# The delta rule's values turned on VectorE and through DRAM, and the diagonal blocks' substitution cut into steps

## The chip, the cores and the metric

One core of a Trainium2 chip runs the whole program. The metric is the device time of one execution in microseconds (us); the kernel before takes 2083.51 us (median of three runs, 2082.48 to 2084.71).

## The reference

One encoder layer on 256 tokens of width 2048, all in f32: a mixer, a cross-attention into 256 memory tokens and a squared-ReLU MLP, each behind an RMSNorm. The mixer has two branches, retention (8 heads) and a gated delta rule (16 heads of 128 keys and 128 values), whose gated outputs are added and projected. The part that the change touches is the delta rule, evaluated in chunks of 64 tokens:

```
gqkv = silu(causal_conv(gqkv, conv_w));  gq, gk, gv = split(gqkv)
gq, gk = l2_normalize(gq) * GDN_DK**-0.5, l2_normalize(gk)
m = where(strict, (k*beta) @ k.T * decay, 0)          # per head and chunk, 64 x 64
t = triangular_solve(eye + m, eye)                    # unit lower triangular
u = t @ (v * beta);  w = t @ (k * beta * exp(cum_g))
v_new = u - w @ state;  o = (q * exp(g)) @ state + (q @ k.T * decay) @ v_new
state = state * exp(g_last) + (k * exp(g_last - g)).T @ v_new
```

## The kernel before

The weights are streamed. `fetch` takes 1 MB of a weight matrix into one of three `raw` buffers by a DMA on SP's queue (L98), and then, for each half of it, ScalarE writes a rounded copy `whi` (L108) and VectorE the remainder `wlo` (L111). Three buffers of each take halves in turn. TensorE multiplies from those: `blocks` (two blocks of 128 output features by all 256 tokens, two matmuls for each block and 128 inputs, L193 and L194) and `chunk` (128 tokens by 512 features, three matmuls, L151 to L153). A fetch of `blocks` feeds 16 pairs of L193 and L194. After each half `blocks` and `chunk` call `step()`, which runs the first generator in the list `steps` up to its next `yield`; `finish_steps()` runs all to their ends. The order in which each engine takes its instructions is set when the program is built, by a planner that goes by priorities and by times of its own; weights' DMAs, roundings and remainders have the highest priority there.

The mixer runs four groups (`j` = 0 to 3; four delta-rule heads and two retention heads each), in a loop at the end of the mixer: `gdn_stream(j)`, `gdn_blocks`, for `j` over 0 `gate_delta_rule(j - 1)`, then `retention(j)` and `gate_retention(j)`. The delta rule's core `gdn_core(j)` is a generator whose steps run inside `gate_retention(j)`, for group 0 inside `gdn_stream(1)`.

`gdn_stream` works on two pairs of heads. For each pair `blocks` runs over the columns of q, k and v; each result goes through `conv_silu` (a scaled copy on ScalarE, L566, three multiply-adds on VectorE, L569, SiLU on ScalarE, L571). The values `vt` come out with features on partitions and tokens along the row. q and k go through Gram matmuls (L614 to L618), from which `alt` is made (L638, L641), and small copies on ScalarE spread its blocks over `cmp_l`, `pair32` and `pair64` (L646 to L653). For each head TensorE turns `vt` by two transposes into PSUM (L657), and ScalarE evacuates them, scaled by the key's norm `nk`, into `r4`, tokens on partitions (L660).

`gdn_blocks` inverts the 32x32 diagonal blocks of all four heads at once: `cmp_l` goes through DRAM into `lw` (L667, L670), VectorE substitutes 31 columns, two instructions each (L678, L680), on 32 partitions, and the result `tw` goes through DRAM into `ct` (L682, L688), is turned by VectorE's 32x32 transposes into `cu` (L690) and copied into `t64`, `u64` and `u128`. It is called once, and its instructions stand together behind `gdn_stream` in the program. `gdn_core` combines the blocks (L709 and on) and multiplies by `r4` (L742 and on).

Of the kernel before, what the change touches and what calls it, by code (L numbers as in the profile page):

```python
# [17 lines left out]
P = 128  # L18
D = 2048
S = 256  # L20
# [31 lines left out]
def trunk(ctx: ExitStack, tc: tile.TileContext, x, mem, positions, norm_mix_g, w_in, conv_w, gdn_a_log, gdn_dt_bias,  # L52
# [508 lines left out]
    t64, u64, u128 = sparse("t64", 64), sparse("u64", 64), sparse("u128", NT, P)  # L561


    def conv_silu(blk, ps, dst):
        acc = mx.tile([P, S], F32, name="acc", tag="acc", bufs=2)
        act.activation(acc, ps, AF.Copy, scale=cw[:, 3, blk:blk + 1])  # L566
        for j in range(2, -1, -1):
            d = 3 - j
            vec.scalar_tensor_tensor(acc[:, d:], ps[:, :S - d], cw[:, j, blk:blk + 1], acc[:, d:],  # L569
                                     op0=ALU.mult, op1=ALU.add)  # L570
        act.activation(dst, acc, AF.Silu)  # L571

    def diag(alt):
        return alt.rearrange("p a n -> p (a n)")[:, 0:512].rearrange("p (t n) -> p t n", t=NT)[:, :, 0:P]
# [1 line left out]
    def gdn_stream(grp):  # L576

        heads = []
        qe4 = mx.tile([P, 4, NT], F32, name="qe4", tag="qe4", bufs=2)
        for pr in range(2):  # L580
            h0 = grp * 4 + pr * 2
            dec = mx.tile([P, 2, 384], F32, name="dec", tag="dec", bufs=1)
            nc.sync.dma_start(dec, dec_d[h0:h0 + 2].rearrange("h p n -> p h n"))
            kq = mx.tile([P, 2, 2, S], F32, name="kq", tag="kq", bufs=1)
            vts = []
            for part, c0, bofs in ((1, C_GQ, 0), (0, C_GK, 16), (2, C_GV, 32)):
                def evac(b, ps, part=part, bofs=bofs):
                    if part < 2:
                        conv_silu(bofs + h0 + b, ps, kq[:, b, part, :])
                    else:  # L590
                        vt = mx.tile([P, S], F32, name="vt", tag="vt", bufs=2)
                        conv_silu(bofs + h0 + b, ps, vt)
                        vts.append(vt)
                blocks(h1, w_in[0], c0 + h0 * GD, 2, evac)
            if pr == 0:
                finish_steps()
                cmp_l = mx.tile([P, 8, 32], F32, name="cmp_l", tag="cmp", bufs=1)
                r4 = mx.tile([P, 4, NT, GD], F32, name="r4", tag="r4", bufs=1)
            grams = []
            ssk = mx.tile([P, 2, NT], F32, name="ssk", tag="ssk", bufs=2)  # L600
            for b in range(2):
                kh = mx.tile([P, 2, S], F32R, name="kh", tag="kh", bufs=2)
                kl = mx.tile([P, 2, S], F32R, name="kl", tag="kl", bufs=2)
                sq = mx.tile([P, S], F32, name="sq", tag="acc", bufs=2)
                act.activation(kh, kq[:, b], AF.Copy)
                vec.tensor_sub(kl, kq[:, b], kh.bitcast(F32))
                act.activation(sq, kq[:, b, 1], AF.Square)
                g0, g1 = bank(), bank()
                g0v = g0.rearrange("p (a n) -> p a n", a=2)
                g1v = g1[:, 0:256].rearrange("p (a n) -> p a n", a=2)  # L610
                if b == 0:
                    ssq = g1[:, 256:260].rearrange("p (b i) -> p b i", b=2)
                for t in range(NT):
                    pe.matmul(ssq[:, b, t:t + 1], sq[:, t * P:(t + 1) * P], ones[:, :1], start=True, stop=True)  # L614
                for n, (l, r) in enumerate(((kh, kh), (kh, kl), (kl, kh))):
                    pe.matmul(g0v, l[:, 0, 0:P], r, start=n == 0, stop=n == 2)  # L616
                for n, (l, r) in enumerate(((kh, kh), (kh, kl), (kl, kh))):
                    pe.matmul(g1v, l[:, 0, P:S], r[:, :, P:S], start=n == 0, stop=n == 2)  # L618
                grams.append((g0v, g1v))
                for t, src in enumerate((g0v[:, 0, 0:P], g1v[:, 0, :])):  # L620
                    dj = sm.tile([P, S], F32, name="dj", tag="bo", bufs=2)[:, :P]
                    vec.scalar_tensor_tensor(dj, src, 1.0, ident, op0=ALU.mult, op1=ALU.mult,
                                             accum_out=ssk[:, b, t:t + 1])
            ske = mx.tile([P, 2, NT], F32, name="ske", tag="ske", bufs=2)
            vec.tensor_scalar(ske, ssk, EPS, None, op0=ALU.add)
            vec.tensor_scalar(qe4[:, 2 * pr:2 * pr + 2, :], ssq, EPS * GD, EPS * EPS * GD,
                              op0=ALU.mult, op1=ALU.add)
            sc = mx.tile([P, 2, NT], F32, name="sc", tag="sc", bufs=2)
            vec.reciprocal(sc, ske)
            vec.tensor_mul(sc, sc, beta[:, :, h0:h0 + 2].rearrange("p t h -> p h t"))  # L630
            nk = mx.tile([P, 2, NT], F32, name="nk", tag="nk", bufs=2)
            pool.tensor_tensor(nk.rearrange("p b t -> p (b t)"), ske.rearrange("p b t -> p (b t)"), half_pow[:, :4], op=ALU.pow)
            for b in range(2):
                h, slot = h0 + b, pr * 2 + b
                g0v, g1v = grams[b]

                alt = mx.tile([P, 2, 384], F32, name="alt", tag="alt", bufs=4)
                vec.scalar_tensor_tensor(alt[:, :, 0:S], g0v, sc[:, b, 0:1],  # L638
                                         dec[:, b, 0:256].unsqueeze(1).to_broadcast([P, 2, 256]),
                                         op0=ALU.mult, op1=ALU.mult)  # L640
                vec.scalar_tensor_tensor(alt[:, :, S:384], g1v, sc[:, b, 1:2],  # L641
                                         dec[:, b, 256:384].unsqueeze(1).to_broadcast([P, 2, P]),
                                         op0=ALU.mult, op1=ALU.mult)
                for q in range(4):
                    ps_ = slice(32 * q, 32 * q + 32)
                    act.activation(cmp_l[ps_, 2 * slot:2 * slot + 2, :], diag(alt)[ps_, :, 32 * q:32 * q + 32], AF.Copy)  # L646

                for t in range(NT):
                    for a in range(2):
                        to, at = 64 * t + 32 * a, 64 * a  # L650
                        act.activation(pair32[to:to + 32, slot, to:to + 32],
                                       diag(alt)[at:at + 32, t, at + 32:at + 64], AF.Copy)
                    act.activation(pair64[64 * t:64 * t + 64, slot, 64 * t:64 * t + 64], diag(alt)[0:64, t, 64:P], AF.Copy)  # L653

                vps = bank()
                for t in range(NT):
                    pe.transpose(vps[:, t * P:(t + 1) * P], vts[b][:, t * P:(t + 1) * P], ident)  # L657
                r = r4[:, slot, :, :]
                for t in range(NT):
                    act.activation(r[:, t, :], vps[:, t * P:(t + 1) * P], AF.Copy, scale=nk[:, b, t:t + 1])  # L660
                heads.append(alt)
        return heads, cmp_l, r4, qe4

    def gdn_blocks(heads, cmp_l):

        scr_l = dram.tile([P, 256], F32, name="scr_l", tag="scr_l", bufs=2)
        nc.sync.dma_start(scr_l, cmp_l.rearrange("p g n -> p (g n)"))  # L667
# [3 lines left out]
        tw = mx.tile([32, 32, 32], F32, name="tw", tag="tw", bufs=1)  # L671
        vec.memset(tw, 0.0)
        vec.memset(tw.rearrange("p i c -> p (i c)")[:, ::33], 1.0)
        for j in range(31):
            n = 31 - j
            pr = mx.tile([32, 272], F32, name="pr", tag="pr", bufs=2)
            pv = pr[:, :n * (j + 1)].rearrange("p (i c) -> p i c", i=n)
# [7 lines left out]
        for t in range(NT):  # L685
            for a in range(2):
                at = 64 * t + 32 * a
                nc.sync.dma_start(ct[at:at + 32], scr_t[16 * a + t:16 * a + 16:2, :].rearrange("g (i c) -> i g c", i=32))  # L688
        cu = mx.tile([P, 8, 32], F32, name="cu", tag="cu", bufs=1)
        vec.transpose(cu.rearrange("p g c -> p (g c)"), ct.rearrange("p g c -> p (g c)"))  # L690
        for t in range(NT):
            for w in range(2):
# [3 lines left out]
                for a in range(2):  # L696
                    at, to = 64 * t + 32 * a, 64 * a + 32 * w
                    act.activation(u128[to:to + 32, :, t, to:to + 32], cu[at:at + 32, 4 * w:4 * w + 4, :], AF.Copy)
        return ct, cu

    def gdn_core(ct, cu, heads, r4, qe4, yg):

        def couple(lhs, rhs, n):
# [3 lines left out]
                pe.matmul(pv[:, i, :], lhs[:, i, :], rhs[:, i, :], start=True, stop=True)  # L709
            return ps, pv  # L710

        ps, pv = couple(pair32, ct[:, 0:4], 32)
        for at in range(0, P, 32):
            (act.copy if at < 64 else vec.tensor_copy)(pair32[at:at + 32, :, at:at + 32], pv[at:at + 32])
        yield
        ps, pv = couple(pair32, cu[:, 4:8], 32)
        nu = mx.tile([P, 2, P], F32, name="nu", tag="g_w", bufs=1)
        vec.tensor_scalar(nu[:, 0], ps, -1.0, None, op0=ALU.mult)
# [161 lines left out]
    gate_retention, gate_delta_rule = gates()  # L880
    for j in range(5):
        if j < 4:
            heads, cmp_l, r4, qe4 = gdn_stream(j)
            solved = gdn_blocks(heads, cmp_l)
        if j:
            if j < 4:
                quad = mx.tile([P, 4, S], F32, name="mg", tag="mg", bufs=3)
# [5 lines left out]
        if j < 4:  # L893
            yr = mx.tile([P, NT, 512], F32, name="yr", tag="yr", bufs=1)
            yg = mx.tile([P, NT, 512], F32, name="yg", tag="yg", bufs=1)
            retention(j, yr)
            core = gdn_core(*solved, heads, r4, qe4, yg)
            if j:
                steps.append(core)
            gate_retention(j, yr)  # L900
# [216 lines left out]
```

## Time and profile before

| | us |
|---|---|
| median of three runs (range) | 2083.51 (2082.48 to 2084.71) |
| the profiled execution, its own time | 2083.63 |
| its span, first to last instruction | 2081.9 |
| TensorE busy in the span | 2064.7 |
| VectorE busy | 1400.9 |
| ScalarE busy | 1119.2 |

The profile is one execution recorded by the hardware profiler. Matmuls are pipelined: the record of one is longer than the distance to the next one's start, so what a matmul costs is read from the distance between starts, and the busy time of a group counts overlapped time in full. A wait is time in which an engine was idle before an instruction, put down to the work that released it. Idle time of an engine off the path costs nothing. Stages: memory tokens and set-up up to about 190 us, the mixer's four groups up to about 1060, output projection and cross-attention up to 1350, the MLP behind it.

### The profile page before, as it was taken

How to read it: one execution, taken by the hardware profiler on the slowest of the kernel's cores; microseconds unless marked ns; L12 is line 12 of the kernel's file. 1: busy time of each engine (PE TensorE's matmuls, PEld its weight loads, DVE VectorE, ACT ScalarE, POOL GpSimd, SP SyncE). 2: the span in 40 equal slices, each digit the busy share in tenths (PEclk: the TensorE clock that was granted, in tenths of full speed). 3: DMA queues.
4: the chain of work that ended last, by engine and by line, in shares of the span. 5: the costliest groups of instructions: out<-in, count | busy, mean ns of one | idle time of the engine just before them, and what ended most of it. 6: DMA issues, size and time to landing. Idle time of an engine off the chain costs nothing.

```text
span 2081.9 us, 28577 instructions
## 1 busy us (share of the span) xinstructions
PE 2064.7 (99%) x11028; PEld 1780.3 (86%) x11028; DVE 1400.9 (67%) x2226; ACT 1119.2 (54%) x1843; POOL 30.7 (1%) x37
## 2 busy tenths in 40 slices
PE   8999999999999999999999999999999999999998
PEld 6888888888888888888888899888888888888887
DVE  5766879778757885778557665766556546645655
ACT  7684664675547555655446564654444434434444
POOL 0000000000000000000000000000000000000000
PEclk9999999999999999999999999999999999999999
DMA  8787655556555655555467654666566556656653
GB/s 297 236 273 251 196 190 195 168 177 196 185 163 189 195 177 166 186 187 190 155 213 238 193 190 144 187 198 195 190 195 189 194 190 192 192 196 188 193 192 142
DMA packets 314168, 405.11 MB, mean 195 GB/s; under 512 B 18336, under 2 KB 222128, under 8 KB 313904
## 3 DMA queue, kind: packets, MB, share of 16 engines
q1 hardware_dynamic: 313744, 402.77, 60.1%
q8 instruction: 86, 1.41, 0.3%
q10 hardware_dynamic: 288, 0.52, 0.1%
q14 instruction: 50, 0.41, 0.1%
HBM read 389.61 MB, written 13.65 MB: 194 GB/s over the span
## 4 chain that ended last, share of the span: by engine, by line
PE 97%; DMA 1%; ACT 1%; SPq 1%; DVE 0%; issue 0%; POOLq 0%; POOL 0%; ACTq 0%; DVEq 0%
PE s L193 33%; PE s L194 17%; PE s L152 14%; PE s L153 14%; PE s L151 14%; PE b L709 1%; PE b L616 1%; DMA xc<-x 1%; PE b L742 1%; PE b L122 0%; PE b L121 0%; PE b L123 0%; SPq L312 0%; ACT dec_w L521 0%; PE b L618 0%
## 5 line engine op out<-in xcount | busy, mean ns | idle before, releaser
L111 DVE TENSOR_TENSOR wlo<-raw,whi 128x1024 fp32r<-128x1024 f32 x700 | 855.4, 1223 | 515.4 <-ACT whi L108 508.9
L108 ACT ACTIVATE whi<-raw 128x1024 fp32r<-128x1024 f32 x700 | 740.7, 1059 | 689.1 <-PE s L153 342.8
L193 PE MATMUL s<-q,whi 128*128 128x512 f32 x3072 | 1056.8, 390 | 0.3 <-DVE q L1006 0.3
L194 PE MATMUL s<-q,wlo 128*128 128x256 f32 x3072 | 840.6, 281 | 0.8 <-DVE wlo L111 0.8
L193 PEld LDWEIGHTS s<-q,whi 128*128 128x128 f32 x3072 | 567.7, 188 | 109.9 <-DVE q L1006 0.5
L194 PEld LDWEIGHTS s<-q,wlo 128*128 128x128 f32 x3072 | 576.2, 188 | 14.2 <-DVE wlo L111 2.6
L152 PE MATMUL s<-wlo,q 128*128 128x512 f32 x1264 | 495.8, 392 | 0.7 <-DVE wlo L111 0.7
L153 PE MATMUL s<-whi,q 128*128 128x512 f32 x1264 | 492.1, 390 | 0.0
L151 PE MATMUL s<-whi,q 128*128 128x512 f32 x1264 | 451.5, 390 | 2.8 <-ACT q L275 2.8
L151 PEld LDWEIGHTS s<-whi,q 128*128 128x128 f32 x1264 | 237.3, 188 | 52.1 <-ACT q L275 3.2
L152 PEld LDWEIGHTS s<-wlo,q 128*128 128x128 f32 x1264 | 237.7, 188 | 49.5 <-DVE wlo L111 2.2
L153 PEld LDWEIGHTS s<-whi,q 128*128 128x128 f32 x1264 | 237.7, 188 | 47.5
L200 ACT ACTIVATE bo<-s 128x256 f32<-128x256 f32 x192 | 72.8, 379 | 119.4 <-PE s L194 106.2
L201 DVE TENSOR_TENSOR bo<-bo,s 128x256 f32<-128x256 f32 x192 | 80.0, 417 | 44.8 <-ACT bo L200 44.4
L569 DVE SCALAR_TENSOR_TENSOR acc<-bo,cw,acc 128x255 f32<-128x255 f32 (+1 forms) x144 | 66.8, 480 | 3.1 <-ACT acc L566 1.2
L678 DVE TENSOR_TENSOR pr<-lw,tw 32x31 f32<-32x31 f32 (+15 forms) x124 | 40.5, 326 | 10.4 <-DMA lw<-scr_l 8.3
L680 DVE TENSOR_TENSOR tw<-tw,pr 32x31 f32<-32x31 f32 (+15 forms) x124 | 40.6, 327 | 2.0
L1045 DVE SCALAR_TENSOR_TENSOR res<-s,rstd3q,res 128x512 f32<-128x512 f32 (+1 forms) x32 | 22.3, 736 | 11.9 <-PE s L153 11.9
L843 ACT ACTIVATE gth<-s 128x512 f32<-128x512 f32 x32 | 19.0, 592 | 20.3 <-PE s L153 15.1
L1034 DVE SCALAR_TENSOR_TENSOR hs<-bo 128x256 f32<-128x256 f32 x64 | 27.1, 423 | 1.1
L1037 DVE TENSOR_TENSOR q<-hs,q 128x256 fp32r<-128x256 f32 x64 | 26.8, 418 | 0.8 <-ACT q L1036 0.8
L1036 ACT ACTIVATE q<-hs 128x256 fp32r<-128x256 f32 x64 | 26.2, 410 | 0.0
(306 smaller groups left out, 1083.6 us busy)
## 6 DMA issues: line engine op xcount, KB each, us to landing
raw<-w_in SPq DMA_DIRECT2D x143, 1024.0 KB
raw<-w_ff SPq DMA_DIRECT2D x128, 1024.0 KB
raw<-w_xkv SPq DMA_DIRECT2D x31, 1024.0 KB
raw<-w_out SPq DMA_DIRECT2D x16, 1024.0 KB
raw<-w_xq SPq DMA_DIRECT2D x16, 1024.0 KB
raw<-w_xo SPq DMA_DIRECT2D x16, 1024.0 KB
dec_d<-dec_w SPq DMA_DIRECT2D x8, 384.0 KB
dec<-dec_d SPq DMA_DIRECT2D x8, 384.0 KB
```

The source lines that it names most:

```text
L108: rounding = act.activation(hi, src, AF.Copy)
L111: vec.tensor_sub(lo, src, hi.bitcast(F32))
L151: pe.matmul(o, xh, wh, start=first, stop=False)
L152: pe.matmul(o, xh, wl, start=False, stop=False)
L153: pe.matmul(o, xl, wh, start=False, stop=last)
L193: pe.matmul(ps[b], lh, xhl, start=kk == 0, stop=False)
L194: pe.matmul(ps[b][:, :S], ll, xh, start=False, stop=kk == KT - 1)
L200: act.activation(o, ps[b][:, S:], AF.Copy)
L201: vec.tensor_add(o, o, ps[b][:, :S])
L569: vec.scalar_tensor_tensor(acc[:, d:], ps[:, :S - d], cw[:, j, blk:blk + 1], acc[:, d:], op0=ALU.mult, op1=ALU.add)
L678: vec.tensor_mul(pv, lw[:, j, j + 1:32].unsqueeze(2).to_broadcast([32, n, j + 1]), tw[:, j, 0:j + 1].unsqueeze(1).to_broadcast([32, n, j + ...
L680: vec.tensor_sub(tw[:, j + 1:32, 0:j + 1], tw[:, j + 1:32, 0:j + 1], pv)
```

## The change

`conv_silu` gets a flag for the values: SiLU is written back into `acc`, and VectorE's 32x32 transposes (`vec.transpose`, 128x256) put each 32x32 block, turned in itself, into `vt`. Four DMAs for a pair of heads write `vt` into a DRAM tile `v_d` with the blocks in their places, and one DMA reads it back into `r4` with tokens on partitions. TensorE's transposes (L657), their PSUM bank and ScalarE's evacuations (L660) go. The scaling by `nk` is done later, by eight ScalarE instructions on `r4` in the second step of `gdn_core`; `nk` of both pairs is kept in `nk4`. `gdn_blocks` becomes a generator that is put into `steps`; it yields twice ahead of the first column, before every third column and twice after the DMAs into `ct`, and hands its results to `gdn_core` through the list `solved`.

```diff
-    def conv_silu(blk, ps, dst):
+    def conv_silu(blk, ps, dst, blocks_of=False):
...
-        act.activation(dst, acc, AF.Silu)
+        act.activation(acc if blocks_of else dst, acc, AF.Silu)
+        if blocks_of:
+            vec.transpose(dst, acc)
...
+        nk4 = mx.tile([P, 4, NT], F32, name="nk4", tag="nk4", bufs=2)
...
-            vts = []
+            vt = mx.tile([P, 2, S], F32, name="vt", tag="vt", bufs=1)
...
-                        vt = mx.tile([P, S], F32, name="vt", tag="vt", bufs=2)
-                        conv_silu(bofs + h0 + b, ps, vt)
-                        vts.append(vt)
+                        conv_silu(bofs + h0 + b, ps, vt[:, b], blocks_of=True)
...
+            v_d = dram.tile([2, S, GD], F32, name="v_d", tag="v_d", bufs=2)
+            for a in range(4):
+                nc.sync.dma_start(v_d[:, :, 32 * a:32 * a + 32].rearrange("h (b i) f -> i (h b) f", i=32),
+                                  vt[32 * a:32 * a + 32].rearrange("i h (b f) -> i (h b) f", f=32))
+            nc.sync.dma_start(r4[:, 2 * pr:2 * pr + 2], v_d.rearrange("h (t p) f -> p h t f", p=P))
...
-                vps = bank()
-                for t in range(NT):
-                    pe.transpose(vps[:, t * P:(t + 1) * P], vts[b][:, t * P:(t + 1) * P], ident)
-                r = r4[:, slot, :, :]
-                for t in range(NT):
-                    act.activation(r[:, t, :], vps[:, t * P:(t + 1) * P], AF.Copy, scale=nk[:, b, t:t + 1])
...
-    def gdn_blocks(heads, cmp_l):
+    def gdn_blocks(cmp_l, solved):
...
+        yield
+        yield
         for j in range(31):
+            if j % 3 == 2:
+                yield
...
                 nc.sync.dma_start(ct[at:at + 32], scr_t[16 * a + t:16 * a + 16:2, :].rearrange("g (i c) -> i g c", i=32))
+        yield
+        yield
...
-        return ct, cu
+        solved.extend((ct, cu))
+        yield
...
+        ct, cu = solved
         ps, pv = couple(pair32, ct[:, 0:4], 32)
...
         yield
+
+        for i in range(4):
+            for t in range(NT):
+                act.activation(r4[:, i, t, :], r4[:, i, t, :], AF.Copy, scale=nk4[:, i, t:t + 1])
...
-            solved = gdn_blocks(heads, cmp_l)
+            solved = []
+            steps.append(gdn_blocks(cmp_l, solved))
...
-            core = gdn_core(*solved, heads, r4, qe4, yg)
+            core = gdn_core(solved, heads, r4, nk4, qe4, yg)
```

## Rows read from the trace of the kernel before

**Rows 1.** Windows by stage: stretch, length, busy us of engines, granted clock, DMA share, GB/s.
```profile
0.00:190.00 190.00, 181.08 (x913) 150.11 (x914) 124.16 (x204) 129.27 (x263) 2.67 (x9) 1.00 0.82 268
190.00:1060.00 870.00, 870.00 (x4624) 749.52 (x4623) 654.29 (x1210) 496.61 (x898) 25.55 (x24) 1.00 0.56 183
```

**Rows 2.** Waits of TensorE, whole span: who waited for whom, us in total, times, longest.
```profile
PE s L194 <- DVE wlo L111: 0.8, 2, 0.4
```

**Rows 3.** Timeline of TensorE at one head pair's transposes: start, us, line, tiles, count.
```profile
255.74 0.39 PE L193 MATMUL s<-q,whi 128*128 128x512 f32 x1
...
256.08 0.39 PE L193 MATMUL s<-q,whi 128*128 128x512 f32 x1
256.31 0.38 PE L657 MATMUL b<-ident,vt 128*128 128x128 f32 x2
...
256.99 0.38 PE L657 MATMUL b<-ident,vt 128*128 128x128 f32 x2
257.13 0.48 PE L193 MATMUL s<-q,whi 128*128 128x512 f32 x1
...
257.56 0.39 PE L193 MATMUL s<-q,whi 128*128 128x512 f32 x1
```

**Rows 4.** Groups by line: count, busy us, mean ns of one, idle before and its releaser.
```profile
L657 PE MATMUL b<-ident,vt 128*128 128x128 f32 x32 | 6.1, 271 | 0.0
...
L660 ACT ACTIVATE r<-b,nk 128x128 f32<-128x128 f32 x32 | 9.6, 366 | 0.1
...
L690 DVE STREAM_TRANSPOSE cu<-ct 128x256 f32<-128x256 f32 x4 | 1.8, 445 | 0.1
```

**Rows 5.** Timeline of ScalarE behind the Gram matmuls, group 0's first pair.
```profile
254.42 1.06 ACT L108 ACTIVATE whi<-raw 128x1024 fp32r<-128x1024 f32 x1
...
257.72 0.62 ACT L660 ACTIVATE r<-b,nk 128x128 f32<-128x128 f32 x2
...
260.55 1.06 ACT L108 ACTIVATE whi<-raw 128x1024 fp32r<-128x1024 f32 x1
```

**Rows 6.** Timeline of VectorE, at the values' convolution and behind Rows 5.
```profile
246.97 1.22 DVE L111 TENSOR_TENSOR wlo<-raw,whi 128x1024 fp32r<-128x1024 f32 x1 [1.15 <-ACT whi L108]
249.56 0.29 DVE L622 SCALAR_TENSOR_TENSOR dj<-b,ident 128x128 f32<-128x128 f32 x1 [1.37 <-PE b L616]
...
261.64 1.22 DVE L111 TENSOR_TENSOR wlo<-raw,whi 128x1024 fp32r<-128x1024 f32 x1 [2.17 <-ACT whi L108]
```

**Rows 7.** Timeline of TensorE: the first matmuls that read that remainder.
```profile
263.56 0.40 PE L194 MATMUL s<-q,wlo 128*128 128x256 f32 x2
```

**Rows 8.** Waits of SP's DMA queue, mixer (190 to 1060 us).
```profile
SPq L98 <- DVE wlo L111: 303.5, 60, 9.5
...
SPq L688 <- DMA scr_t<-tw: 11.6, 4, 4.0
...
SPq L670 <- DMA scr_l<-cmp_l: 6.2, 4, 3.4
```

**Rows 9.** Timeline of SP: transfers issued around the end of a substitution, and one fetch.
```profile
313.57 0.39 SPq L98 DMA_DIRECT2D raw<-w_in  x1
...
363.27 0.83 SPq L688 DMA_DIRECT2D ct<-scr_t  x2
...
530.29 0.34 SPq L682 DMA_DIRECT2D scr_t<-tw  x1
534.73 1.79 SPq L688 DMA_DIRECT2D ct<-scr_t  x4
```

**Rows 10.** Windows of one us: DMA share and GB/s at the ends of two transfers.
```profile
317.00:318.00 1.00, 1.00 (x7) 0.88 (x6) 0.90 (x4) 0.55 (x1) 0.00 (x0) 1.00 1.03 384
318.00:319.00 1.00, 1.00 (x6) 0.83 (x5) 1.00 (x2) 0.51 (x1) 0.00 (x0) 1.00 0.12 40
...
537.00:538.00 1.00, 1.00 0.54 80
```

**Rows 11.** Timeline of TensorE: the core of group 0 begins.
```profile
371.42 0.97 PE L709 MATMUL b<-ct,pair 128*128 128x32 f32 x8
```

More of the change, by code (lines that the diff above doesn't have):

```diff
@@ L630, in gdn_stream @@
             vec.tensor_mul(sc, sc, beta[:, :, h0:h0 + 2].rearrange("p t h -> p h t"))
-            nk = mx.tile([P, 2, NT], F32, name="nk", tag="nk", bufs=2)
+            nk = nk4[:, 2 * pr:2 * pr + 2, :]
             pool.tensor_tensor(nk.rearrange("p b t -> p (b t)"), ske.rearrange("p b t -> p (b t)"), half_pow[:, :4], op=ALU.pow)
@@ L653, in gdn_stream @@
                     act.activation(pair64[64 * t:64 * t + 64, slot, 64 * t:64 * t + 64], diag(alt)[0:64, t, 64:P], AF.Copy)
-                vps = bank()
-                for t in range(NT):
-                    pe.transpose(vps[:, t * P:(t + 1) * P], vts[b][:, t * P:(t + 1) * P], ident)
-                r = r4[:, slot, :, :]
-                for t in range(NT):
-                    act.activation(r[:, t, :], vps[:, t * P:(t + 1) * P], AF.Copy, scale=nk[:, b, t:t + 1])
                 heads.append(alt)
-        return heads, cmp_l, r4, qe4
-    def gdn_blocks(heads, cmp_l):
+        return heads, cmp_l, r4, nk4, qe4
+    def gdn_blocks(cmp_l, solved):
         scr_l = dram.tile([P, 256], F32, name="scr_l", tag="scr_l", bufs=2)
@@ L698, in gdn_blocks, with gdn_core @@
                     act.activation(u128[to:to + 32, :, t, to:to + 32], cu[at:at + 32, 4 * w:4 * w + 4, :], AF.Copy)
-        return ct, cu
-    def gdn_core(ct, cu, heads, r4, qe4, yg):
+        solved.extend((ct, cu))
+        yield
+    def gdn_core(solved, heads, r4, nk4, qe4, yg):
         def couple(lhs, rhs, n):
@@ L882, in trunk @@
         if j < 4:
-            heads, cmp_l, r4, qe4 = gdn_stream(j)
-            solved = gdn_blocks(heads, cmp_l)
+            heads, cmp_l, r4, nk4, qe4 = gdn_stream(j)
+            solved = []
+            steps.append(gdn_blocks(cmp_l, solved))
         if j:
```

## Prediction

> **What bounds the kernel now.** I read the windows by stage first. In the mixer (190 to 1060 us), the only stage that the change touches, TensorE is busy 870.00 of 870.00 us at a granted clock of 1.00, while VectorE has 654.29, ScalarE 496.61 and the DMA engines a share of 0.56 [rows 1]. Overlapping records can hide small holes, so the list of TensorE's waits comes next: over the whole span its waits on VectorE's remainders come to 0.8 us in two waits [rows 2], and the same list cut to the mixer is empty. So in this stage the end is set by the sum of TensorE's own instructions, and nothing that VectorE, ScalarE or the DMAs give up shortens it. Two things count: how many us of TensorE's row the change takes away, and whether anything that it adds makes a weight half come late. The third reading is therefore TensorE's timeline where the removed transposes stand [rows 3], and the last ones are the places where a half is nearly late [rows 5 to 7] and SP's waits, behind which the weights are fetched [rows 8, 9].
>
> **What is removed from TensorE.** 32 transposes (4 groups, 2 pairs, 2 heads, 2 token halves). Their cost is read as distances between starts. Without anything in between, a pair of L193 and L194 takes from 255.74 to 256.08, 0.34 us. From 256.08 to 257.56 there are three pairs and four transposes in 1.48 us [rows 3]. Three pairs alone take 1.02, so four transposes with both returns to the weights' stream cost 0.46, or 0.115 each. The start at 257.13 shows that part of it is the return: that matmul's record is 0.48 long beside 0.39 for the others. The other heads stand in the stream in the same way. 32 x 0.115 = **3.7 us** less. The upper end is the group's busy time, 6.1 us [rows 4], which counts overlap with the neighbours in full; the lower end is 0, if something else comes late. I take the distances, since they are what TensorE's row is made of.
>
> The record of one transpose is 271 ns [rows 4]. The Trainium skill (TensorE: Matmul & The Clock Gate, Part 4: PE-mode transpose) gives some 275 ns for one in a kernel's context, and the trace agrees as a duration; by that price the estimate would be 32 x 0.275 = 8.8 us, and by the distances of rows 3 it is 3.7.
>
> **ScalarE.** 32 evacuations of 366 ns go (9.6 us busy [rows 4]), 32 scalings of the same 128x128 shape come, read from SBUF. No row shows this form from SBUF; its ends are the rounding's pace, 1.06 us for 1024 columns [rows 5], so 0.13 for 128, and the evacuation's own 366 ns, and I take the latter, so nothing is won or lost in sum. Their place is better than before: between two roundings at 254.42 and 260.55 [rows 5] ScalarE does only small copies for 5 us, among them four of the removed evacuations in two rows of 0.62. The remainder behind it starts at 261.64 and ends at 262.86, and TensorE wants it at 263.56 [rows 6, 7]: 0.7 us to spare, among the tightest places of the mixer. The change takes 1.2 us out of that burst. The eight scalings land in the core's second step, 8 x 0.366 = 2.9 us; if they stood in one piece ahead of a rounding with 0.7 us to spare they would cost 2.2 us once, in group 0, whose core runs among convolutions. Roundings have the higher priority, so I take 0, and 2.2 for the range.
>
> **VectorE.** 16 transposes of 128x256 at 445 ns (the same form as L690 [rows 4]) add 7.1 us to 654. They fall at the values' convolution, where VectorE stands idle for 1.15 and 1.37 us in front of two instructions [rows 6]; that is the cover for two times 0.445. A transpose now waits for the SiLU on ScalarE, and behind it on VectorE's queue are remainders: without the cover a pair would lose 0.9 us less the slack, up to 0.2 us for each of 8 pairs, 1.6 in all. I take 0.
>
> **SP and the DMAs.** For each pair five transfers come into SP's queue behind the values, 40 in all: four of 64 KB in runs of 128 bytes (512 runs each), and the load of `r4`, which waits for all four. While it waits, the fetches behind it in SP's queue wait too, and so, later, roundings and TensorE. How long: the four `ct` loads, 4 x 256 runs of 128 bytes, start at 534.73 [rows 9] and their traffic ends within the window that ends at 538 [rows 10], 3.3 us. Twice as many runs take between 3.3 us (if latency is most of it) and 6.6. The room: a fetch issued at 313.57 [rows 9] has its bytes in by about 318.2, where a share of 0.12 is left [rows 10], so 4.6 us; two other buffers hold 2 x 16 x 0.34 = 11 us of work, so SP can be late by about 6.4. The kernel before has such blocks already, on `scr_t` up to 4.0 us and on `scr_l` up to 3.4 [rows 8], and TensorE waits for none of them; SP mostly waits for buffers to come free, up to 9.5 us at a time. Cost 0; at the upper end 8 x 0.2 = 1.6 us. The traffic itself, 8 times at most 6.6 us and 256 KB of reading, meets a DMA share of 0.56.
>
> **The substitution in parts.** The same 62 VectorE instructions a group, spread by hand over the 16 steps of `retention(0)` or `gate_delta_rule`, where the planner now spreads them. Nothing is removed from TensorE; price 0. Who waits is the core: group 0's `ct` loads are issued at 363.27 and its first matmul starts at 371.42 [rows 9, 11], 8 us later. The two empty steps at each end shift this by at most 4 steps of 8 pairs, 4 x 8 x 0.34 = 11 us, 3 beyond the slack, if the columns in between run no earlier; they are placed earlier than that (the 16 steps end with `retention(0)`, a `gate_retention` before the core), so 0, and 3 for the range. In groups 1 to 3 a whole `retention` lies in between. The steps' yields cost no engine time.
>
> **Sum.** 2083.63 us of the profiled execution less 3.7 = **2079.9**; this execution lies 0.1 above the median. That is 0.17% below, just under the 0.2% (4.2 us) that a measurement of this kernel can tell from no change.
>
> **Rivals.**
> 1. *The gain is eaten by small waits.* VectorE's 1.6, ScalarE's 2.2 and a part of SP's 1.6 come true instead of 0: 2079.9 + 3.1 to 5.4, about 2083.5. For it: spare times of 0.7 us; against it: an empty list of waits today although ScalarE's burst was longer.
> 2. *Weights come late behind the new load on SP.* Place: the fetch behind `r4`'s load, 8 times. Rows show runs of 128 bytes only into SBUF; written to DRAM they may be dearer. At one and a half times the 6.6 us the block is 9.9, 3.5 beyond the room, 8 x 3.5 = 28 us: 2108. It decides from (4.2 + 3.7) / 8 = 1.0 us beyond the room, a block of 7.4 us. Against it: fetches have the higher priority when the planner orders SP's queue, and the blocks of today, up to 4.0 us [rows 8], cost nothing. The Trainium skill (DMA: Bandwidth & Descriptors, Specifications) has a rule for this side: below 512 bytes a transfer is read, modified and written. No run here shows a write of that size yet.
> 3. *Removing a transpose gives more than its distance.* By the busy time of 6.1 us the time is 2077.5; by the full records, 32 x 0.271 = 8.7 us, it is 2074.9. Against it: the neighbours run under those records. The skill's duration named above would give the same as the records.
> 4. *The change does not do what it says*: the steps alter nothing, since the planner had spread the columns already. That is in the forecast.
>
> **How the numbers follow.** Forecast 0.67, of which 0.20 falls on the far side of 4.2 us, as the price of a transpose need only be 0.131 instead of 0.115, or the runs differ by half a us (the three runs span 2.2 us); rival 1 0.12; rival 2 0.10; rival 3 0.11. Faster by over 0.2%: 0.20 + 0.11 = 0.31; within: 0.47 + 0.12 = 0.59; slower: 0.10. The range takes in the busy time of 6.1 less half a us for the runs' spread below (2077.0) and rival 1 above (2084.0); it leaves out rival 2 and the far part of rival 3.
>
> **What would show it.** In the profile after: TensorE's busy time and matmul count down by some 6 us overlapped and 32; the distances around the convolutions back at 0.34; TensorE's list of waits in the mixer still empty (a row for L194 or L152 on `wlo` is rival 1, one with roundings waiting for a `raw` DMA is rival 2); SP's waits gaining a row of eight waits on `v_d`, each under 6.4 us; transposes of 0.445 us on VectorE. The prediction is wrong if TensorE's instructions in the mixer get shorter by other than 3 to 4.5 us, or if it waits there for over 1 us.

## The result and the profile after

| | us |
|---|---|
| before, median of six runs | 2083.52 |
| changed, median of six runs (range) | 2094.31 (2091.77 to 2096.13) |
| ratio | 1.005, 95% interval 1.004 to 1.006 |
| changed, the profiled execution | 2091.77, span 2090.0 |

The change makes the kernel 10.8 us slower; the forecast was 3.6 us faster. The profiled execution is the fastest of the six, 8.1 us of span above that of before.

Windows by stage (columns as in rows 1) show where it lies:

```profile
0.00:190.00 190.00, 181.31 (x919) 150.31 (x920) 124.44 (x204) 129.25 (x264) 2.74 (x9) 1.00 0.83 270
190.00:1070.00 880.00, 871.25 (x4594) 746.27 (x4593) 660.64 (x1226) 496.97 (x899) 24.59 (x24) 1.00 0.58 186
```

The stage up to 190 us is as before [rows 1]. In the mixer TensorE, which had no idle time at all, now stands idle for 880 - 871.25 = 8.75 us. VectorE has 6 us more to do than before and ScalarE as much as before (661 and 497 us). TensorE's list of waits, cut to the mixer, was empty and now reads:

```profile
PE s L193 <- ACT whi L108: 2.4, 3, 1.3
PE s L194 <- DVE wlo L111: 2.1, 4, 0.5
PE s L152 <- DVE wlo L111: 2.1, 3, 0.8
PE s L151 <- ACT whi L108: 2.0, 1, 2.0
```

Four of the eleven waits are for the rounded copy itself, which ScalarE makes, not only for VectorE's remainder behind it. So the next view is what ScalarE waited for in the mixer (us in total, times, longest). The row that was not there before:

```profile
ACT r L727 <- DMA r<-v_d: 10.8, 7, 3.0
```

L727 is the scaling of `r4`. It stands in the second step of `gdn_core` in the program, for group 0 over 100 us later (the core begins at 371.42 in rows 11). The timeline of ScalarE shows where it runs, and what stands behind it, at the two pairs of group 0 (the counterpart of rows 5):

```profile
254.99 0.26 ACT L660 ACTIVATE pair<-alt 64x64 f32<-64x64 f32 x1
256.79 1.28 ACT L727 ACTIVATE r<-r,nk 128x128 f32<-128x128 f32 x4 [1.54 <-DMA r<-v_d]
...
258.60 1.04 ACT L108 ACTIVATE whi<-raw 128x1024 fp32r<-128x1024 f32 x1
...
263.71 1.06 ACT L108 ACTIVATE whi<-raw 128x1024 fp32r<-128x1024 f32 x1
```

```profile
295.24 1.28 ACT L727 ACTIVATE r<-r,nk 128x128 f32<-128x128 f32 x4 [2.59 <-DMA r<-v_d]
296.43 1.04 ACT L108 ACTIVATE whi<-raw 128x1024 fp32r<-128x1024 f32 x1
...
302.98 1.06 ACT L108 ACTIVATE whi<-raw 128x1024 fp32r<-128x1024 f32 x1
```

The planner put four scalings into ScalarE's queue right at the burst of small copies behind the Gram matmuls, at the place where the evacuations had been. There ScalarE waits 1.54 and 2.59 us for the load of `r4`, and everything behind stands: the copies, and then the roundings. TensorE pays at the other end of that queue. Its timeline, and VectorE's, at the second pair:

```profile
301.66 0.39 PE L153 MATMUL s<-whi,q 128*128 128x512 f32 x1
304.09 0.73 PE L151 MATMUL s<-whi,q 128*128 128x512 f32 x2 [2.04 <-ACT whi L108]
305.35 0.50 PE L152 MATMUL s<-wlo,q 128*128 128x512 f32 x1 [0.53 <-DVE wlo L111]
305.69 0.40 PE L153 MATMUL s<-whi,q 128*128 128x512 f32 x1
```

```profile
304.07 1.23 DVE L111 TENSOR_TENSOR wlo<-raw,whi 128x1024 fp32r<-128x1024 f32 x1 [2.16 <-ACT whi L108]
```

The rounding begun at 302.98 ends at 304.04, L151 starts at 304.09; its remainder ends at 305.30, L152 starts at 305.35. What TensorE loses there is 2.04 + 0.53 us, and what the records hide: the record of the matmul before a wait is 0.39 us and not the usual distance of 0.23, and the first matmul behind a wait is followed only after 0.34 (305.35 to 305.69).

SP's side of the load, timeline and waits, and VectorE's remainder at that time:

```profile
247.17 0.37 SPq L98 DMA_DIRECT2D raw<-w_in  x1
247.63 3.36 SPq L603 DMA_DIRECT2D v_d<-vt  x4
254.00 0.38 SPq L605 DMA_DIRECT2D r<-v_d  x1
256.26 0.39 SPq L98 DMA_DIRECT2D raw<-w_in  x1
```

```profile
SPq L605 <- DMA v_d<-vt: 25.6, 15, 4.0
```

```profile
255.02 1.22 DVE L111 TENSOR_TENSOR wlo<-raw,whi 128x1024 fp32r<-128x1024 f32 x1
```

SP waits for the writes for at most 4.0 us at a time, and no row has ScalarE waiting for a `raw` DMA in the mixer. The load of `r4` is issued from 254.00 and has landed by 256.79, where L727 starts. SP is done with it at 254.38, and the next fetch starts at 256.26, just as a remainder ends (256.24), which is what frees a buffer: SP was not late there.

### The profile page after: what moved, and what is told of

It reads as the page before. It is cut to its first block, busy times and chain, and to the rows that moved or that the text cites. A ratio compares the mean times of both kernels' runs of the same rounds, so it can differ in the third digit from the quotient of the medians.

```text
span 2090.0 us, 28585 instructions
## 1 busy us (share of the span) xinstructions
PE 2064.4 (99%) x10996; PEld 1775.9 (85%) x10996; DVE 1406.4 (67%) x2242; ACT 1117.7 (53%) x1843; POOL 29.8 (1%) x37
## 4 chain that ended last, share of the span: by engine, by line
PE 89%; DMA 4%; ACT 3%; DVE 1%; SPq 1%; issue 1%; POOLq 0%; POOL 0%; ACTq 0%; DVEq 0%
PE s L193 31%; PE s L194 16%; PE s L152 13%; PE s L153 13%; PE s L151 13%; DMA v_d<-vt 1%; ACT whi L108 1%; DVE wlo L111 1%; DMA r<-v_d 1%; PE b L716 1%; DMA lw<-scr_l 1%; DMA xc<-x 1%; PE b L754 1%; PE b L122 0%; PE b L121 0%
## 5 line engine op out<-in xcount | busy, mean ns | idle before, releaser
L193 PE MATMUL s<-q,whi 128*128 128x512 f32 x3072 | 1057.4, 390 | 2.7 <-ACT whi L108 2.4
L194 PE MATMUL s<-q,wlo 128*128 128x256 f32 x3072 | 840.8, 281 | 2.9 <-DVE wlo L111 2.8
L193 PEld LDWEIGHTS s<-q,whi 128*128 128x128 f32 x3072 | 567.7, 188 | 114.5 <-ACT whi L108 3.7
L194 PEld LDWEIGHTS s<-q,wlo 128*128 128x128 f32 x3072 | 576.1, 188 | 17.8 <-DVE wlo L111 6.7
L152 PE MATMUL s<-wlo,q 128*128 128x512 f32 x1264 | 495.5, 392 | 2.6 <-DVE wlo L111 2.6
L151 PE MATMUL s<-whi,q 128*128 128x512 f32 x1264 | 451.2, 390 | 4.5 <-ACT q L275 2.5
L151 PEld LDWEIGHTS s<-whi,q 128*128 128x128 f32 x1264 | 236.9, 188 | 54.1 <-ACT q L275 2.9
L152 PEld LDWEIGHTS s<-wlo,q 128*128 128x128 f32 x1264 | 237.6, 188 | 52.7 <-DVE wlo L111 5.3
```

The costliest lines, as they stand in the source:

```text
L151: pe.matmul(o, xh, wh, start=first, stop=False)
L152: pe.matmul(o, xh, wl, start=False, stop=False)
L193: pe.matmul(ps[b], lh, xhl, start=kk == 0, stop=False)
L194: pe.matmul(ps[b][:, :S], ll, xh, start=False, stop=kk == KT - 1)
```

## The experiments

The theory: the scalings, placed early by the planner, wait at the head of ScalarE's queue for a load from DRAM, and the roundings behind them come late. Rival A: the load holds SP up, so that the weights come late. Rival B: the substitution in steps delays VectorE. Ratios are against the kernel before in the same runs (2083.76 us for the first four kernels, 2083.32 for the rest).

### The scalings left out

```diff
-        for i in range(4):
-            for t in range(NT):
-                act.activation(r4[:, i, t, :], r4[:, i, t, :], AF.Copy, scale=nk4[:, i, t:t + 1])
```

> The changed kernel without the eight scalings of r4 on ScalarE (the values stay unscaled, so part of the computation is left out); transposes, transfers and steps stay. Theory: the planner put the scalings in front of roundings, where they wait for the load of r4, and the roundings behind them come late; without them the time is that of the forecast, about 2080 us (2083.5 less 3.7), and TensorE waits for no rounding in the mixer. Rival A (SP held up by the load of r4, so that weights come late): the load stays, so about 2094. Rival B (the substitution in steps delays VectorE): about 2094.

Measured: 2081.41 us, ratio 0.999 (0.998 to 0.9999). Transfers, transposes and steps are all there, TensorE waits for nothing in the mixer, and the 10.8 us are gone. Rivals A and B fall as causes of the loss.

### The scalings tied to their place

`behind` is ScalarE's last copy in the core's first step; the scalings may not come ahead of it in ScalarE's queue.

```diff
-            (act.copy if at < 64 else vec.tensor_copy)(pair32[at:at + 32, :, at:at + 32], pv[at:at + 32])
+            made = (act.copy if at < 64 else vec.tensor_copy)(pair32[at:at + 32, :, at:at + 32], pv[at:at + 32])
+            if at < 64:
+                behind = made.ins
...
-        for i in range(4):
-            for t in range(NT):
-                act.activation(r4[:, i, t, :], r4[:, i, t, :], AF.Copy, scale=nk4[:, i, t:t + 1])
+        with tc.issue_after(behind):
+            for i in range(4):
+                for t in range(NT):
+                    act.activation(r4[:, i, t, :], r4[:, i, t, :], AF.Copy, scale=nk4[:, i, t:t + 1])
```

> The changed kernel with the scalings tied, in ScalarE's order, behind the copies of the core's first step, where the program text has them; nothing is left out. Theory: about 2080 us, faster than before by 3 to 4.5 us, no row of ScalarE waiting for the load of r4. Rivals A and B: about 2094, since transfers and steps are the same.

Measured: 2081.04 us, ratio 0.9986 (0.9977 to 0.9995): 13.3 us below the changed kernel and 2.7 below the kernel before, with nothing changed but the order in which ScalarE takes its work. The group of the scalings, and TensorE's window in the mixer, of this kernel:

```profile
L730 ACT ACTIVATE r<-r,nk 128x128 f32<-128x128 f32 x32 | 9.8, 390 | 0.1
```

```profile
190.00:1060.00 870.00, 869.98 (x4601) 747.91 (x4600) 661.85 (x1227) 498.58 (x900) 23.33 (x24) 1.00 0.61 188
```

As many instructions of the same length, but with 0.1 us of idle time in front of them instead of 10.8, and TensorE is full again, without a wait in the mixer.

### The substitution in steps alone

The kernel before with `gdn_blocks` as a generator, its yields and `solved`, and nothing else of the change.

```diff
...
-            solved = gdn_blocks(heads, cmp_l)
+            solved = []
+            steps.append(gdn_blocks(cmp_l, solved))
...
```

> The kernel before with the substitution in steps alone; the values are still turned by TensorE. Theory: the steps cost and bring nothing, 2083.5 us within 1.5. Rival B: slower, some 2090 to 2094.

Measured: 2083.86 us, ratio 1.0 (0.9991 to 1.0009). This half of the change does nothing to the time.

### The transposes left out of the kernel before

```diff
-                vps = bank()
-                for t in range(NT):
-                    pe.transpose(vps[:, t * P:(t + 1) * P], vts[b][:, t * P:(t + 1) * P], ident)
...
-                    act.activation(r[:, t, :], vps[:, t * P:(t + 1) * P], AF.Copy, scale=nk[:, b, t:t + 1])
+                    act.activation(r[:, t, :], vts[b][:, t * P:(t + 1) * P], AF.Copy, scale=nk[:, b, t:t + 1])
```

> The kernel before without TensorE's 32 transposes: ScalarE scales the values as they are from SBUF into r4 (they stay unturned, so part of the computation is left out). It prices the removal alone. Theory: 32 x 0.115 = 3.7 us less, 2079.8. By the busy time of the group 2077.4, by the whole records 2074.8.

Measured: 2080.35 us, ratio 0.9984 (0.9975 to 0.9993), 3.4 us less. The distances between starts gave 3.7; busy time (6.1) and whole records (8.7) lie outside the interval of this run (1.5 to 5.2 us less).

It says something on the theory too. ScalarE's scalings from SBUF stand early here as well, and they wait at the head of its queue for `nk` from GpSimd, for longer in sum than in the changed kernel:

```profile
ACT r L657 <- POOL nk L632: 14.6, 4, 3.7
```

TensorE still waits for only 0.4 us in the mixer. ScalarE's timeline at group 1's second pair, in the kernel before and here, shows why:

```profile
460.55 0.47 ACT L651 ACTIVATE pair<-alt 32x32 f32<-32x32 f32 x2 [3.67 <-DVE alt L638]
```

```profile
459.10 1.28 ACT L657 ACTIVATE r<-vt,nk 128x128 f32<-128x128 f32 x4 [3.65 <-POOL nk L632]
```

The wait stands where ScalarE was idle anyway, for `alt`. The kernel before has a row of 11.0 us in three such waits, and this one has none left (at the fourth place it had stood idle for a matmul, 4.02 us). The changed kernel keeps that row, and its waits for the load come on top:

```profile
ACT pair L658 <- DVE alt L645: 10.1, 3, 3.4
```

So it is not any wait at the head of the queue that costs, but one in a stretch where ScalarE had work to do.

### The values alone, the substitution in one piece

```diff
-            steps.append(gdn_blocks(cmp_l, solved))
+            for _ in gdn_blocks(cmp_l, solved):
+                pass
```

> The changed kernel with the substitution in one piece again, values still turned through DRAM, scalings where the planner puts them. Theory: the wait for the load of r4 in front of the roundings is all of it, so the time stays at 2092 to 2096 us. Rival B (the steps have a part in it): nearer to 2081.

Measured: 2093.83 us, ratio 1.0051 (1.0037 to 1.0065). All of the loss is in the values' half. ScalarE's row on the load is the same, 10.6 us in 7 waits.

### The wait without the work

```diff
-                act.activation(r4[:, i, t, :], r4[:, i, t, :], AF.Copy, scale=nk4[:, i, t:t + 1])
+                act.activation(r4[:, i, t, 0:1], r4[:, i, t, 0:1], AF.Copy, scale=nk4[:, i, t:t + 1])
```

> The changed kernel with the scalings cut to one column each (the other columns of r4 stay unscaled, a part that is left out): the same eight instructions at the same places on ScalarE wait for the load of r4, but nearly without work. Theory: it is the wait that holds the roundings up, not the 1.28 us of scaling per pair (the kernel before has as long evacuations there), so most of the loss stays: 2088 to 2093 us. If the work were the cause: about 2081.

Measured: 2089.99 us, ratio 1.0034 (1.0023 to 1.0045). ScalarE's row:

```profile
ACT r L727 <- DMA r<-v_d: 11.1, 7, 2.9
```

The wait is the same, and it keeps 2089.99 - 2081.04 = 9.0 of the 13.3 us that lie between the changed kernel and the tied one. The other 4.3 are near to what the work became shorter by: one instruction takes 280 ns instead of 388, 32 x 0.108 = 3.5 us. (The medians of both kernels also hold what the clock took, see the last section.) So wait and work add up in this burst; with work alone (the evacuations of before) it just fitted. The changed kernel shows it at the one pair without a wait, group 1's first. There the four scalings stand in one piece ahead of the rounding, where two of the four evacuations stood before, and TensorE waits 0.53 us for a remainder:

```profile
433.60 1.28 ACT L727 ACTIVATE r<-r,nk 128x128 f32<-128x128 f32 x4
434.79 1.04 ACT L108 ACTIVATE whi<-raw 128x1024 fp32r<-128x1024 f32 x1
```

```profile
437.14 0.51 PE L194 MATMUL s<-q,wlo 128*128 128x256 f32 x2 [0.53 <-DVE wlo L111]
```

### Tied, without the steps

```diff
-            steps.append(gdn_blocks(cmp_l, solved))
+            for _ in gdn_blocks(cmp_l, solved):
+                pass
```

(on the version with the scalings tied)

> The version with the scalings tied behind the core's first step, and the substitution in one piece; nothing left out. Theory: the steps bring nothing here either, 2081.0 us within 1 of the version with steps. Rival: the steps free ScalarE or VectorE near the core, then some us slower than that version.

Measured: 2080.72 us, ratio 0.9988 (0.998 to 0.9997). The steps bring nothing there either; this and the tied version with steps are the two that beat both kernels, and nothing here tells them apart.

### The transfers twice

On the tied version, the four writes and the load of each pair are done twice.

```diff
-            v_d = dram.tile([2, S, GD], F32, name="v_d", tag="v_d", bufs=2)
-            for a in range(4):
...
-            nc.sync.dma_start(r4[:, 2 * pr:2 * pr + 2], v_d.rearrange("h (t p) f -> p h t f", p=P))
+            for again in range(2):
+                v_d = dram.tile([2, S, GD], F32, name="v_d", tag="v_d", bufs=2)
+                for a in range(4):
...
+                nc.sync.dma_start(r4[:, 2 * pr:2 * pr + 2], v_d.rearrange("h (t p) f -> p h t f", p=P))
```

> The version with the scalings tied, and each pair's four writes of the values and the load of r4 done twice, one chain behind the other: SP waits twice for the writes. It measures how much room SP's queue has. Theory: the room of about 6.4 us before the weights come late holds for one chain; with two (waits up to 2 x 4 us, most of them with a fetch between) the loss is small, 2081 to 2084 us. Rival A (weights close to late already): 8 x 2 us or more, 2097 and up.

Measured: 2082.35 us, ratio 0.9995 (0.9985 to 1.0004). That is 1.3 us above the tied version, and 1.6 above the tied one without steps of the same runs. TensorE's waits in the mixer are one row, and SP's timeline at the first pair follows:

```profile
PE s L152 <- DVE wlo L111: 1.0, 1, 1.0
```

```profile
247.53 6.33 SPq L604 DMA_DIRECT2D v_d<-vt  x8
254.11 3.31 SPq L606 DMA_DIRECT2D r<-v_d  x2
257.46 0.50 SPq L98 DMA_DIRECT2D raw<-w_in  x1
```

SP is held for 9.9 us here, from 247.53 to 257.42. So SP's queue has room for twice what the change puts there. Rival A was far from deciding.

## Why the prediction was wrong

**The step that failed** is the paragraph on ScalarE: "The eight scalings land in the core's second step". That is their place in the program, and I took it for their place in ScalarE's queue. The planner orders each engine by times of its own. The scalings need only `r4` and `nk`, so by those times they were ready early, and it put them there (the place is shown by the trace; the planner's reckoning is inferred from it), into the very burst that the prediction had named as the tightest place (0.7 us to spare, [rows 5 to 7]). On the chip the load landed up to 3.0 us after ScalarE had come to them, 1.5 in the mean of seven waits. TensorE, whose waits the prediction put at nothing, waited 8.6 us in the mixer. "Roundings have the higher priority" did not help: priority chooses among what the planner takes to be ready, and a queue, once written, is taken in order. Of VectorE's transposes and SP's load I asked what stands behind them where they become ready. Of the scalings I asked it only for a place 100 us later, and there only for their work (2.2 us once), not for a wait.

**What the sum was worth.** The removal: 3.7 forecast, 3.4 measured alone. The burst: "takes 1.2 us out" was wrong, since work of 1.28 us came to the same place with a wait of 10.8 / 7 = 1.5 us on top. In the profiled execution TensorE's 8.75 us of idle time in the mixer, less 3.4 for the transposes, make 5.3 of the 8.1 us. The rest is what the records hide: at each of the eleven waits 0.39 - 0.23 = 0.16 us in front and 0.34 - 0.23 = 0.11 behind, 3.0 in all, by the distances at the second pair; that makes 8.3. The median lies another 2.5 us above the profiled execution, which is the fastest of the six; the last section has what points to the clock for it.

**Rivals.** Rival 2 had the right transfer and the wrong engine: it looked at SP behind the load of `r4` and not at the instruction that reads `r4`. Its own sum does not hold either. SP is held for 254.00 - 247.63 = 6.4 us before the load goes out at the first pair, the upper end of the forecast 3.3 to 6.6 and all of the room of 6.4, and no fetch was late there. With the transfers twice it is held for 9.9, which by that sum is 8 x 3.5 = 28 us, and 1.3 were measured. The room was sized too small; at the first pair the fetch behind had to wait for its buffer in any case (until 256.24). The 0.10 for a slower kernel was all given to this rival. Rival 1 named late remainders from ScalarE's burst, but as 2.2 us once, in group 0; ScalarE waited in seven bursts of eight. (Its sum reaches 2079.9 + 5.4 = 2085.3, beyond the 2084.0 at which the prediction ends its range.) Rival 3 is out by measurement. Rival 4, that the steps do nothing, is confirmed on both versions.

**Smaller steps.** VectorE's transposes cost nothing, as forecast: 438 ns each, and in the tied version TensorE is full with them in place. The short runs written to DRAM: the four writes take SP 3.36 us to issue, more than the 1.8 for the four `ct` loads [rows 9]; the rule on short transfers of the Trainium skill (DMA: Bandwidth & Descriptors, Specifications), whose effect these runs can't separate from latency, did not decide here.

**What stays open.** With the scalings tied the gain is 2.7 us, not 3.4, though the two intervals overlap. In that kernel some stretches run at a slightly longer distance, without any wait: at 272 us, pairs of L193 and L194 follow each other by 0.35 to 0.36 us instead of the 0.34 of rows 3, from its timeline of TensorE:

```profile
272.22 0.40 PE L193 MATMUL s<-q,whi 128*128 128x512 f32 x1
272.46 0.28 PE L194 MATMUL s<-q,wlo 128*128 128x256 f32 x1
272.58 0.40 PE L193 MATMUL s<-q,whi 128*128 128x512 f32 x1
272.81 0.28 PE L194 MATMUL s<-q,wlo 128*128 128x256 f32 x1
272.93 0.40 PE L193 MATMUL s<-q,whi 128*128 128x512 f32 x1
```

The kernel before has such stretches as well, but fewer. Over the mixer the mean distance of these pairs, from the timelines of TensorE, is 0.3467 us before (864 pairs) and 0.3484 in the tied version (879), 1.5 us in all, so it is large enough for the missing 0.7. In the kernel without the transposes it is 0.3455, so that some 1 us of its 3.4 may be this and not the transposes' own time. What makes it was not tried.

## What to carry to other kernels

The place of an instruction in the program is not its place in an engine's queue when a planner orders the queue: when a change makes an instruction ready early, price it where it becomes ready, and ask what stands behind it there if its data come later than planned. Data that now come by DMA instead of from an engine turn such an instruction into a wait at the head of an in-order queue; tie it behind the work that it is for. On an engine far from full (ScalarE at 57% of the mixer), look at the tightest burst, not at the share: it had 0.7 us to spare, and 10.8 us of waits put into such bursts came out as 8.6 us of waits on TensorE. A wait that stands where the engine was idle anyway is free: 14.6 us of them on ScalarE cost TensorE 0.4.

## What the runs showed of the hardware

After some of the waits TensorE's granted clock fell. In the profiled execution of the version with the values alone, windows around the second pair's wait (columns as in rows 1), and TensorE's timeline there:

```profile
302.00:305.00 3.00, 1.54 (x7) 0.94 (x5) 0.85 (x2) 2.87 (x11) 0.00 (x0) 1.00 0.13 43
305.00:306.00 1.00, 0.43 (x2) 0.30 (x2) 0.45 (x1) 1.00 (x3) 0.00 (x0) 1.00 0.01 1
306.00:307.00 1.00, 0.47 (x3) 0.17 (x2) 1.00 (x2) 1.00 (x2) 0.00 (x0) 1.00 0.30 47
307.00:310.00 3.00, 3.00 (x8) 2.33 (x9) 3.00 (x7) 2.73 (x6) 0.00 (x0) 0.50 0.76 217
310.00:314.00 4.00, 4.00 (x19) 3.27 (x18) 2.75 (x6) 1.27 (x2) 0.00 (x0) 0.95 0.86 281
```

```profile
307.29 0.63 PE L153 MATMUL s<-whi,q 128*128 128x512 f32 x1
307.72 0.63 PE L152 MATMUL s<-wlo,q 128*128 128x512 f32 x1
308.14 0.63 PE L153 MATMUL s<-whi,q 128*128 128x512 f32 x1
```

TensorE had just waited 2.04 and 0.53 us for ScalarE and VectorE. Then the granted clock is 0.50, the lower of its two levels (1.2 GHz), for the whole window from 307 to 310, while the engine is busy throughout, and the distance between matmuls is 0.43 us instead of 0.23. In those 3 us it does what takes 1.6 at full clock, so a late half can cost more than its wait. The same execution has a second such stretch, behind waits of 1.27 and 0.53 us, and the profiled execution of the version with the wait alone has one, behind waits of 1.97 and 0.52 us:

```profile
888.00:889.00 1.00, 1.00 (x5) 0.81 (x4) 1.00 (x3) 1.00 (x3) 0.00 (x0) 0.50 0.71 102
889.00:890.00 1.00, 1.00 (x5) 0.90 (x4) 1.00 (x3) 0.76 (x2) 0.00 (x0) 0.50 0.94 342
```

```profile
306.00:307.00 1.00, 1.00 (x4) 0.76 (x3) 1.00 (x4) 0.99 (x1) 0.00 (x0) 0.50 0.76 131
307.00:308.00 1.00, 1.00 (x4) 0.80 (x3) 1.00 (x3) 0.90 (x3) 0.00 (x0) 0.50 1.03 397
```

The changed kernel's profiled execution, with the same wait at 304.09, kept a clock of 1.00 there and has no such stretch in the mixer. The 5 us at 0.50 of the version with the values alone are an estimated 5 x (1 - 0.23 / 0.43) = 2.3 of the 4.0 us by which its span (2094.0) is longer than that one (2090.0). The mean granted clock of the changed kernel's profiled execution is 0.999, that of its five other executions 0.997 or 0.998, and those are the slower ones (2092.89 to 2096.13 us). That the spread of its times comes from such stretches is likely; those five have no profile that would show it.
